# Down projections with the residual added in halves, an earlier bias table, and the last K and Q parts kept in pages

## The chip, the cores and the metric

The kernel runs on one core of one Trainium2 chip. The metric is the device time of one execution in microseconds (us). TensorE does the matrix products and is called PE in the profile, VectorE is DVE, ScalarE is ACT, GpSimd is POOL, and SyncE, which here only issues DMAs, is SP. A DMA issued from POOL goes through a queue of its own; on the way it can add what it reads to what already stands at the destination, which this kernel uses for the residual.

## The reference

A trunk of two layers over a residual stream `x` of 1024 positions by 1024 channels, all in float32:

```python
for i in range(2):
    h = rms_norm(x, mix_norm[i])
    x = x + (short_conv_mixer(h, ...) if i == 0 else dilated_attention_mixer(h, ..., rel_bias))
    x = x + swiglu(rms_norm(x, ffn_norm[i]), w_gate[i], w_up[i], w_down[i])   # 2816 hidden channels
return rms_norm(x, final_norm)

def swiglu(h, w_gate, w_up, w_down):
    return (jax.nn.silu(h @ w_gate) * (h @ w_up)) @ w_down
```

The attention has 16 heads of 64 and three dilated windows whose outputs are mixed by their log-denominators; each score gets a bias, looked up in the 32x16 table `rel_bias` by distance. FFN0 below is the feed-forward part of layer 0, FFN1 that of layer 1.

## The kernel before

**Numbers as pairs.** Every float32 operand is split in a rounded part `hi` and a rest `lo`, and each product is three matmuls: hi·hi, hi·lo, lo·hi (L612, L613, L614 in `mm`). ACT writes hi (L157 for weights, L604 for activations), DVE then subtracts to get lo (L158, L605). L225 on DVE forms the sums of weight blocks that the scheme below needs.

**Seven products.** The large projections use a seven-product scheme (class `Strassen`). PE does one product after another into one of eight banks; the order of all instructions is written by hand (the program is scheduled by the order of its code), so every engine works its own list in that order and waits by semaphores.

**The down projection.** `down(c, feed)` does chunk `c` of the hidden channels; both feed-forward parts have three chunks here (some tiles are done apart). Chunk by chunk it goes through the products m = 1, 2, 6, 7, 4, 5, 3, and within each through k = 0, 2, 4, 6. Each (m, k) is 9 or 12 matmuls of 128x512 (three for each tile of the chunk: three tiles or four), and its bank is added to one half of one tile of the result, `X[n]` (128x1024, half 0 or 1). m = 1 and 2 go to half 0 of X0, X2, X4, X6; m = 6 and 3 to half 1 of these; m = 4 to half 0 of X1, X3, X5, X7; m = 7 and 5 to half 1 of these. In chunk 0 the first bank for a half is copied by ACT (L836: m = 1, 6, 7, 4) and the second added by DVE (L839: m = 2, 5, 3); in the later chunks DVE adds all of them (L839). So in chunk 0 the half 0 of X0, X2, X4, X6 is complete after m = 2, half 0 of X1, X3, X5, X7 after m = 4, and the other halves after m = 5 and m = 3.

**The residual.** The x of before the feed-forward part lies in DRAM (`source`, called `spill` in the trace). In chunk 0, POOL adds it to a finished X tile by an accumulating DMA (L854). `feed` loads the hidden activations (`hin`, L813 on SP) and splits them for the products to come; `take` does the same for the weights (`raw`, L188 on SP), four products ahead.

**The bias tables.** `bias_tables` is a generator in three steps: (1) DVE fills `rel`, POOL clears and loads five small tiles (`oh` and `rel`, L541 to L549); (2) ACT and DVE split `rel`; (3) PE multiplies them into four banks (L560), ACT and DVE add the two halves of each bank (L561, L562), and the result goes to DRAM (`tables`). `after(m, k)` calls one step at each of three places in the last chunk of FFN0. In the same places `ready_half` squares and splits finished halves of X for the next phase (L1182, L923, L924).

**The Q/K phase.** After FFN0 the Q and K projections run pair by pair (8 pairs). `emit` scales a finished 128x512 part on DVE (L1197, L1199), splits it (ACT L1202, DVE L1205) and stores both pieces to DRAM through POOL (`kq`, L1203 and L1206). While the last of these are stored, PE does the first value tiles of the attention (L1578 to L1580).

**Memory.** Tiles of 128x1024 come from a ring of 41 `page`s that lives all through the kernel. Tiles of 128x512 (`half_page`) come from a pool that is opened anew for each of three stages: the pool of the first stage is closed after the Q/K phase, and the second pool takes its memory. What is loaded into tiles of the second pool (the `bias` tiles of L1529, and behind them on SP's list `ka`, `qa`, `ql`, L1606 to L1612) therefore waits for whoever still uses a half page of the first. PE's first scores (L1634, L1635) read `kca` (made by ACT from `ka`, L1618), `qa` and `ql`.

Of the kernel before, what the change touches and what calls it, by code (L numbers as in the profile page):

```python
# [11 lines left out]
F32R = mybir.dt.float32r  # L12
AF = mybir.ActivationFunctionType
ALU = mybir.AluOpType
# [9 lines left out]
HALF = 512  # L24
# [30 lines left out]
QK_PAIRS = 8  # L55
# [58 lines left out]
def trunk(ctx: ExitStack, tc: tile.TileContext, x, gains_in, cwi, ck, cwo, wqkv, wo, relb,  # L114
          wg, wu, wd, oneh, ident, out):
    nc = tc.nc
# [6 lines left out]
    def page(name, dt=F32):  # L123
        return pages.tile([128, 1024], dt, name=name, tag="page", bufs=PAGES)
# [3 lines left out]
    def half_page(name, dt=F32):  # L128
        return scope["pool"].tile([128, 512], dt, name=name, tag="half", bufs=scope["halves"])

    def bank():
        return psum.tile([128, 512], F32, name="bank", tag="bank")

    def half(h):
        return slice(h * HALF, (h + 1) * HALF)
# [302 lines left out]
    X = [None] * KT  # L438
# [140 lines left out]
    class Strassen:  # L579
# [248 lines left out]
        def down(self, c, feed):  # L828

            p, r, done = {}, {}, set()  # L830

            def add(n, h, b):
                if c == 0 and (n, h) not in done:
                    if X[n] is None:
                        X[n] = page("x")
                    nc.scalar.activation(X[n][:, half(h)], b, AF.Copy)  # L836
                    done.add((n, h))
                else:
                    nc.vector.tensor_tensor(out=X[n][:, half(h)], in0=X[n][:, half(h)], in1=b, op=ALU.add)  # L839

            for i, m in enumerate(DOWN):
                d = c + (i + 2) // len(DOWN)
                steps = range(len(self.chunks[d])) if d < len(self.chunks) else (0, 2)
                for k in range(0, KT, 2):
                    if m == 1:
                        p[k] = bank()
                    if m == 5:
                        r[k] = bank()
                    b = bank() if m == 2 else r[k] if m in (3, 5) else p[k]
                    self.mm((c, k), m, b, m in (1, 2, 5), 4)  # L850
                    n, h = k + (m in (5, 7, 4)), int(m in (6, 5, 7, 3))
                    add(n, h, b)
                    if c == 0 and m in (5, 3):
                        nc.gpsimd.dma_start(out=X[n], in_=self.source[n], accum_op=ALU.add)  # L854
                    if m == 4:
                        del p[k]
                    if k // 2 in steps:
                        next(feed, None)
                    self.downed(c, m, k)

        def downed(self, c, m, k):
            pass
# [301 lines left out]
    class QueryKey(Conv):  # L1164
# [28 lines left out]
        def emit(self, p, part, h, v):  # L1193

            t, rstd = half_page("kq"), self.norm.rstd[:, half(h)]
            if part == 1:
                nc.vector.tensor_tensor(out=by_time(t), in0=by_residue(v), in1=by_residue(rstd), op=ALU.mult)  # L1197
            else:
                nc.vector.scalar_tensor_tensor(t, v, 0.125, rstd, op0=ALU.mult, op1=ALU.mult)  # L1199
            yield  # L1200
            hi, lo, to = half_page("kq_hi", F32R), half_page("kq_lo", F32R), self.kq[p, part]
            nc.scalar.activation(hi, t, AF.Copy)  # L1202
            nc.gpsimd.dma_start(to[:128, half(h)], hi.bitcast(F32))  # L1203
            yield
            nc.vector.tensor_tensor(out=lo, in0=t, in1=hi, op=ALU.subtract)  # L1205
            nc.gpsimd.dma_start(to[128:, half(h)], lo.bitcast(F32))  # L1206
# [89 lines left out]
    class Swiglu(Strassen):  # L1296
# [111 lines left out]
                    self.storing.pop(0)  # L1408

        def downed(self, c, m, k):  # L1410
            if self.after and c + 1 == len(self.chunks):
                self.after(m, k)

        def feed_forward(self, stats, last_step, after, final=None):
            prep, self.after = [], after

# [554 lines left out]
    with tc.tile_pool(name="first", bufs=1) as scope["pool"]:  # L1971
        scope["halves"] = 20
        conv = Conv(Norm(0))
        sw, group1, *rest = into_ffn(0, Norm(2))
        conv.mix(group1)
        norm = Norm(1)
        qk = QueryKey(norm)
        tab = bias_tables()

        def after(m, k):  # L1980
            if (m, k) in ((1, 0), (1, 4), (2, 2)):
                next(tab, None)
            if m in (2, 4, 5, 3):
                qk.ready_half(k + (m in (4, 5)), int(m in (5, 3)), (m, k) in ((2, 0), (5, 0)))
            if m == 3:
                combos[QK, k // 4]((6, 7)[k // 2 % 2])

        sw.feed_forward(*rest, after)
        qk.mix()
# [123 lines left out]
```

## Time and profile before

| | |
|---|---|
| time, median of 3 runs | 2102.26 us (2100.35 to 2102.6) |
| the profiled execution: its time / its span | 2099.16 us / 2097.4 us |
| mean granted PE clock | 0.998 |
| PE busy | 2074.3 us, 99% |
| DVE busy | 1759.1 us, 84% |
| ACT busy | 1027.7 us, 49% |
| POOL busy | 256.0 us, 12% |
| DMA queues: SP's / POOL's share of 16 engines' span | 32.3% / 13.2% |
| FFN0 chunk 0 to 1 / FFN1 chunk 0 to 1 | around 801 / around 1924 us |
| bias tables on PE / first scores of the attention | 893 to 898 / 1136 to 1142 us |

Times in the rows are microseconds from the start of the span. Matmuls are pipelined: the profile gives each 128x512 matmul 0.39 us, but when nothing holds PE they start 0.227 us apart (the stretch from 1893 to 1925 has 143 of them), so lost time on PE is read from how many matmuls a stretch holds, and not from the busy share alone. In a row of the timeline the number in brackets is how long the engine stood idle before it, and what ended that.

### The profile page before, as it was taken

Reading aid. Unit: us, or ns where it says so; the run is one execution under the profiler, and the core shown is the slowest. Engines: PE = TensorE matmul, PEld = TensorE weight load, DVE = VectorE, ACT = ScalarE, POOL = GpSimd, SP = SyncE. Lnnn points to the kernel's source line nnn. Section 1 sums busy time; section 2 is a strip of 40 time slices with the busy share of each in tenths; the row PEclk is TensorE's granted clock in tenths of the full one; section 3 lists DMA queues with packets and bytes.
Section 4 is the critical chain, followed back from the end, with each engine's and each line's share of the span. In section 5 each row is a group of like instructions: output and inputs, shape, how many; then the busy total and the mean of one; then the engine's idle time right before and its main releaser. Section 6 shows DMA issues by size and latency. Waiting matters only on the chain.

```text
span 2097.4 us, 30780 instructions
## 1 busy us (share of the span) xinstructions
PE 2074.3 (99%) x10954; PEld 1785.2 (85%) x10954; DVE 1759.1 (84%) x3302; ACT 1027.7 (49%) x1902; POOL 256.0 (12%) x365
## 2 busy tenths in 40 slices
PE   9999999999999999999999999999999999999998
PEld 7888888888888888878889999998888888887787
DVE  8898769988888887888975888987998888896996
ACT  8433427443444563456543666655544444354443
POOL 1000000110101001010322333211001010001000
PEclk9999999999999999999999999999999999999999
DMA  7322643323323567552757867955223333368532
GB/s 221 96 96 71 236 133 74 106 101 111 109 99 109 174 221 198 174 143 106 241 179 211 195 175 216 244 182 139 81 86 109 100 109 103 114 216 211 162 101 81
DMA packets 131624, 305.69 MB, mean 146 GB/s; under 512 B 15324, under 2 KB 46126, under 8 KB 131472
## 3 DMA queue, kind: packets, MB, share of 16 engines
q1 hardware_dynamic: 96128, 203.51, 32.3%
q0 software_dynamic: 27712, 85.52, 13.2%
q10 hardware_dynamic: 7632, 14.70, 1.9%
q8 instruction: 87, 1.43, 0.3%
q14 instruction: 65, 0.53, 0.1%
HBM read 209.99 MB, written 84.50 MB: 140 GB/s over the span
## 4 chain that ended last, share of the span: by engine, by line
PE 84%; DVE 6%; issue 4%; DMA 2%; POOL 1%; ACT 1%; SPq 0%; POOLq 0%; DVEq 0%; ACTq 0%
PE bank L612 18%; PE bank L614 18%; PE bank L613 18%; PE bank L1709 5%; PE bank L415 3%; PE bank L417 3%; PE bank L416 3%; PE bank L704 3%; PE bank L707 3%; PE bank L706 3%; DMA x<-spill 2%; PE bank L1635 1%; PE bank L1634 1%; PE bank L1578 1%; PE bank L1580 1%
## 5 line engine op out<-in xcount | busy, mean ns | idle before, releaser
L614 PE MATMUL bank<-b,w 128*128 128x512 f32 x2064 | 805.0, 390 | 5.1 <-DVE w L158 4.7
L612 PE MATMUL bank<-b,w 128*128 128x512 f32 x2064 | 804.5, 390 | 3.4 <-ACT w L157 1.7
L613 PE MATMUL bank<-b,w 128*128 128x512 f32 x2064 | 804.0, 390 | 0.4 <-DVE b L924 0.3
L614 PEld LDWEIGHTS bank<-b,w 128*128 128x128 f32 x2064 | 387.4, 188 | 92.7 <-DVE w L158 11.8
L612 PEld LDWEIGHTS bank<-b,w 128*128 128x128 f32 x2064 | 387.6, 188 | 83.6 <-ACT w L157 2.4
L613 PEld LDWEIGHTS bank<-b,w 128*128 128x128 f32 x2064 | 387.6, 188 | 79.9 <-DVE b L924 1.3
L157 ACT ACTIVATE w<-combo 128x512 fp32r<-128x512 f32 (+2 forms) x496 | 258.9, 549 | 267.7 <-DVE combo L225 250.8
L158 DVE TENSOR_TENSOR w<-combo,w 128x512 fp32r<-128x512 f32 (+2 forms) x496 | 286.4, 590 | 32.9 <-ACT w L157 32.6
L618 ACT ACTIVATE part<-bank 128x512 f32<-128x512 f32 x192 | 114.5, 596 | 393.6 <-PE bank L614 390.2
L158 DVE TENSOR_TENSOR w<-raw,w 128x512 fp32r<-128x512 f32 (+2 forms) x340 | 190.6, 582 | 36.8 <-ACT w L157 36.6
L622 DVE TENSOR_TENSOR part<-part,bank 128x256 f32<-128x256 f32 (+1 forms) x372 | 174.9, 499 | 34.7 <-PE bank L614 18.6
L157 ACT ACTIVATE w<-raw 128x512 fp32r<-128x512 f32 (+2 forms) x340 | 171.2, 536 | 26.9 <-PE bank L707 10.5
L415 PE MATMUL bank<-w_hi,w 128*128 128x512 f32 (+1 forms) x336 | 126.2, 376 | 0.0
L839 DVE TENSOR_TENSOR x<-x,bank 128x512 f32<-128x512 f32 x136 | 92.8, 683 | 38.7 <-DMA x<-spill 19.2
L416 PE MATMUL bank<-w_lo,w 128*128 128x512 f32 (+1 forms) x336 | 124.2, 370 | 0.0
L417 PE MATMUL bank<-w_hi,w 128*128 128x512 f32 (+1 forms) x336 | 124.1, 369 | 0.0
L225 DVE TENSOR_TENSOR combo<-raw 128x512 f32<-128x512 f32 (+1 forms) x176 | 116.0, 660 | 0.0
L605 DVE TENSOR_TENSOR b<-hin,b 128x512 fp32r<-128x512 f32 x140 | 95.3, 685 | 15.5 <-ACT b L604 15.4
L534 DVE TENSOR_TENSOR x<-x,bank 128x512 f32<-128x512 f32 (+1 forms) x88 | 55.7, 635 | 41.4 <-PE bank L417 40.6
L604 ACT ACTIVATE b<-hin 128x512 fp32r<-128x512 f32 x140 | 86.0, 618 | 2.6 <-PE bank L614 1.4
L707 PE MATMUL bank<-b,w 128*128 128x256 f32 x288 | 81.5, 283 | 0.0
L706 PE MATMUL bank<-b,w 128*128 128x256 f32 x288 | 81.5, 283 | 0.0
(229 smaller groups left out, 3310.5 us busy)
## 6 DMA issues: line engine op xcount, KB each, us to landing
hin<-part SPq DMA_DIRECT2D x140, 256.0 KB, 3.8
raw<-in_ffn_w_gate SPq DMA_DIRECT2D x44, 512.0 KB, 3.7
raw<-in_ffn_w_up SPq DMA_DIRECT2D x44, 512.0 KB, 3.7
part<-sum POOLq DMA_DIRECT2D x80, 256.0 KB, 2.3
raw<-in_attn_w_qkv SPq DMA_DIRECT2D x27, 512.0 KB, 4.0
raw<-in_conv_w_in SPq DMA_DIRECT2D x24, 512.0 KB, 4.2
raw<-in_ffn_w_down SPq DMA_DIRECT2D x32, 384.0 KB, 5.0
part<-part POOLq DMA_DIRECT2D x40, 256.0 KB, 2.5
```

What stands on the lines that cost most here:

```text
L157: nc.scalar.activation(hi, src, AF.Copy)
L158: low = lambda: eng.tensor_tensor(out=lo, in0=src, in1=hi, op=ALU.subtract)
L225: eng.tensor_tensor(out=c, in0=a, in1=b, op=op)
L415: nc.tensor.matmul(b, whi[:, a], ahi[:, s], start=first, stop=False)
L416: nc.tensor.matmul(b, whi[:, a], alo[:, s], start=False, stop=False)
L417: nc.tensor.matmul(b, wlo[:, a], ahi[:, s], start=False, stop=last)
L612: nc.tensor.matmul(b, hi[:, a], bhi, start=start and k == 0, stop=False, skip_group_check=True)
L613: nc.tensor.matmul(b, hi[:, a], blo, start=False, stop=False, skip_group_check=True)
L614: nc.tensor.matmul(b, lo[:, a], bhi, start=False, stop=k == n - 1, skip_group_check=True)
L622: nc.vector.tensor_tensor(out=t, in0=t, in1=b, op=ALU.add)
L706: nc.tensor.matmul(b, hi[:, a], blo, start=False, stop=False, skip_group_check=True)
L707: nc.tensor.matmul(b, lo[:, a], bhi, start=False, stop=k == n - 1, skip_group_check=True)
```

## The change

Three edits; the arithmetic stays the same.

1. In chunk 0 of each down projection, the residual is added in halves of 128x512, each right after the product that completes the half, and no longer in tiles of 128x1024 after m = 5 and m = 3.
2. The first step of `bias_tables` moves from the last chunk's (1, 0) to (3, 2) of the chunk before, the second from (1, 4) to (1, 2), the third from (2, 2) to (2, 0). For this `after` now gets the chunk too, counted back from the last.
3. In `emit`, the hi and lo pieces of the last Q/K pair lie in the two halves of a page, and no longer in two half pages.

```diff
@@ down
-                    if c == 0 and m in (5, 3):
-                        nc.gpsimd.dma_start(out=X[n], in_=self.source[n], accum_op=ALU.add)
+                    if c == 0 and m in (2, 4, 5, 3):
+                        nc.gpsimd.dma_start(out=X[n][:, half(h)], in_=self.source[n][:, half(h)], accum_op=ALU.add)
@@ emit
-            hi, lo, to = half_page("kq_hi", F32R), half_page("kq_lo", F32R), self.kq[p, part]
+            to = self.kq[p, part]
+            if p == QK_PAIRS - 1:
+                w = page("kq_w", F32R)
+                hi, lo = w[:, :HALF], w[:, HALF:]
+            else:
+                hi, lo = half_page("kq_hi", F32R), half_page("kq_lo", F32R)
@@ downed
-            if self.after and c + 1 == len(self.chunks):
-                self.after(m, k)
+            if self.after:
+                self.after(c + 1 - len(self.chunks), m, k)
@@ the call in layer 0
-        def after(m, k):
-            if (m, k) in ((1, 0), (1, 4), (2, 2)):
+        def after(c, m, k):
+            if (c, m, k) in ((-1, 3, 2), (0, 1, 2), (0, 2, 0)):
                 next(tab, None)
+            if c < 0:
+                return
```

What this does to the order of instructions, at three places. First POOL's list at chunk 0 of FFN0, before (`spill_77` to `spill_84` are the residuals of X0 to X7, `part` a store of the stage before):

```order
L784 DMA part_10_4_240<-sum 128x512
L854 DMA x<-spill_78 128x1024
L854 DMA x<-spill_80 128x1024
L854 DMA x<-spill_82 128x1024
L854 DMA x<-spill_84 128x1024
L854 DMA x<-spill_77 128x1024
L854 DMA x<-spill_79 128x1024
```

And now (first the halves after m = 2, then those after m = 4, then the first of those after m = 5; the others of m = 5 and the four of m = 3 follow):

```order
L784 DMA part_10_4_240<-sum 128x512
L854 DMA x<-spill_77 128x512
L854 DMA x<-spill_79 128x512
L854 DMA x<-spill_81 128x512
L854 DMA x<-spill_83 128x512
L854 DMA x<-spill_78 128x512
L854 DMA x<-spill_80 128x512
L854 DMA x<-spill_82 128x512
L854 DMA x<-spill_84 128x512
L854 DMA x<-spill_78 128x512
```

Eight DMAs became sixteen of half the size, and X0's, which stood fifth, now begins the list. FFN1 reads the same.

Second, DVE's list where the bias tables are made, before:

```order
L158 TENSOR_TENSOR w<-combo,w 128x512
L839 TENSOR_TENSOR x<-x,bank 128x512
L605 TENSOR_TENSOR b<-hin,b 128x512
L924 SCALAR_TENSOR_TENSOR b<-x,gains,b 128x512
L225 TENSOR_TENSOR combo<-raw 128x512
L225 TENSOR_TENSOR combo<-combo,raw 128x512
L158 TENSOR_TENSOR w<-combo,w 128x512
L839 TENSOR_TENSOR x<-x,bank 128x512
L605 TENSOR_TENSOR b<-hin,b 128x512
L562 TENSOR_TENSOR t_8374<-bank,low 16x512
L562 TENSOR_TENSOR t_8374<-bank,low 16x201
```

And now:

```order
L158 TENSOR_TENSOR w<-combo,w 128x512
L839 TENSOR_TENSOR x<-x,bank 128x512
L605 TENSOR_TENSOR b<-hin,b 128x512
L562 TENSOR_TENSOR t_8350<-bank,low 16x512
L562 TENSOR_TENSOR t_8350<-bank,low 16x201
```

One product's share of DVE's work (L924 to L605) has moved from ahead of L562 to behind it; on PE the four L560 stand 12 matmuls sooner.

Third, POOL's list at the end of the Q/K phase, before (`kq_0_2937` and `kq_1_2938` are Q and K of the last pair):

```order
L1203 DMA kq_1_2936<-kq_hi 128x512
L1206 DMA kq_1_2936<-kq_lo 128x512
L1203 DMA kq_0_2937<-kq_hi 128x512
L1206 DMA kq_0_2937<-kq_lo 128x512
L1203 DMA kq_1_2938<-kq_hi 128x512
L1206 DMA kq_1_2938<-kq_lo 128x512
L1546 MEMSET ql_10357 64x1024
```

And now:

```order
L1208 DMA kq_1_2936<-kq_hi 128x512
L1211 DMA kq_1_2936<-kq_lo 128x512
L1208 DMA kq_0_2937<-kq_w 128x512
L1211 DMA kq_0_2937<-kq_w 128x512
L1208 DMA kq_1_2938<-kq_w 128x512
L1211 DMA kq_1_2938<-kq_w 128x512
L1551 MEMSET ql_10361 64x1024
```

The order is the same; the last four transfers now read from pages, so the last one that reads a half page is the `kq_lo` of the pair before.

## The prediction

> **What bounds the kernel now.** PE is busy for 99% of the span, so only the places where PE waits can give time back. I read the list of waits first, for whom PE waited (us in total, times, longest), then the table by stretches, for how many matmuls the suspected ones hold, and then the timeline at each place.
>
> ```profile
> PE bank L614 <- DVE w L158: 4.7, 8, 1.3
> PE bank L560 <- issue: 2.5, 1, 2.5
> PE bank L1635 <- DMA raw<-in_attn_w_qkv: 1.7, 1, 1.7
> PE bank L612 <- DVE t L562: 0.8, 1, 0.8
> PE bank L1634 <- ACT kca L1618: 0.5, 1, 0.5
> ...
> 1925.00:1957.00 32.00, 29.27 (x121) 21.55 (x120) 23.35 (x43) 8.70 (x18) 0.00 (x0) 1.00 0.64 148
> 1957.00:1989.00 32.00, 32.00 (x143) 26.48 (x142) 29.51 (x54) 15.17 (x32) 0.00 (x0) 1.00 0.63 205
> 803.00:835.00 32.00, 31.61 (x137) 25.04 (x136) 23.37 (x38) 7.26 (x13) 0.00 (x0) 1.00 0.65 162
> 893.00:906.00 13.00, 9.71 (x43) 7.70 (x42) 11.37 (x23) 9.23 (x19) 2.14 (x4) 1.00 0.38 93
> ```
>
> In the lower rows the stretch comes first, then its length, then busy time (and instructions) of PE, PEld, DVE, ACT, POOL, then the granted clock. An undisturbed 32 us holds 143 matmuls, 0.227 us apart. The start of FFN1's second chunk (1925 on) holds 22 fewer, 5.0 us; that of FFN0 (803 on) 6 fewer, 1.4 us. The bias tables' 13 us hold 39 large matmuls and four L560 where 58 belong: 19 × 0.227 = 4.3, less some 0.6 of L560's own work, 3.7 us. The attention's start loses 3.9 us (below). Together 14.0 us, the most that this change can touch.
>
> **Residual in halves.** DVE is what PE waits for at the chunk crossings, and DVE itself waits for the residual's DMAs. Its waits from 780 to 830 and from 1924 to 1960, its timeline there, and the longest PE wait behind it:
>
> ```profile
> DVE x L839 <- DMA x<-spill: 9.8, 3, 7.1
> ...
> DVE x L839 <- DMA x<-spill: 9.4, 4, 7.6
> ...
> 808.80 0.69 DVE L839 TENSOR_TENSOR x<-x,bank 128x512 f32<-128x512 f32 x1 [7.11 <-DMA x<-spill]
> ...
> 1931.72 0.69 DVE L839 TENSOR_TENSOR x<-x,bank 128x512 f32<-128x512 f32 x1 [7.65 <-DMA x<-spill]
> ...
> 1934.26 0.69 DVE L839 TENSOR_TENSOR x<-x,bank 128x512 f32<-128x512 f32 x1 [0.78 <-DMA x<-spill]
> ...
> 1936.72 0.69 DVE L839 TENSOR_TENSOR x<-x,bank 128x512 f32<-128x512 f32 x1 [0.71 <-DMA x<-spill]
> ...
> 1939.60 0.50 PE L614 MATMUL bank<-b,w 128*128 128x512 f32 x1 [1.20 <-DVE w L158]
> ```
>
> Chunk 1's first add was due at 808.80 − 7.11 = 801.7 in FFN0 and 1931.72 − 7.65 = 1924.1 in FFN1. DVE works in order: behind the add stand L605 and L158, and these make PE late. The add touches half 0 of X0 alone, whose residual now leaves some 40 us sooner. Half 1 is first wanted at m = 6, eight products later: 801.7 + 8 × 2.72 = 823.5 (12 matmuls each) and 1924.1 + 8 × 2.04 = 1940.4 (9 matmuls). Are the halves there by then?
>
> ```profile
> x<-spill POOLq DMA_DIRECT2D x16, 512.0 KB, 13.5
> acc<-sq POOLq DMA_DIRECT2D x15, 256.0 KB, 3.8
> acc<-sq POOLq DMA_DIRECT2D x6, 512.0 KB, 5.1
> ...
> DMA to landing us min/median/max: 3.3/4.1/6.6
> ...
> 786.75 0.90 POOL L854 DMA_DIRECT2D x<-spill  x1 [38.19 <-DMA raw<-in_ffn_w_down]
> ...
> L836 ACT ACTIVATE x<-bank x7: 598/598/600, 771.2 to 783.5; 128x512 f32<-128x512 f32 x7
> L836 ACT ACTIVATE x<-bank x6: 598/598/598, 1896.4 to 1906.6; 128x512 f32<-128x512 f32 x6
> ```
>
> The first three rows are DMA issues (KB each, median us to landing), the fourth all landings of the 256 KB accumulating DMAs of L1187. Queued 512 KB residuals land about 2.5 us apart (the DVE rows 1931.72, 1934.26, 1936.72). The halves are half the bytes; between the two sizes of `acc<-sq` lie 5.1 − 3.8 = 1.3 us. So I take 1.3 to 1.6 us for a queued half, 3.3 to 6.6 us for one alone. The last m = 4 copies start at 783.5 and 1906.6, so these four leave from about 777 and 1900; 12 halves in line from there take 12 × 1.6 = 19 us and are through by 796 and 1919, or, since the last of them leave only as chunk 1 begins (801 and 1924), some 4 us after that; due are 823 and 1940. POOL pays eight more issues of 0.90 us in each FFN, where it stood idle for 38 us. What follows once this wait is gone: chunk 1's DVE work on its own. The crossing to chunk 2 has the same adds and splits and no residual, and its row (1957 on) has the full 143. So the gain is 5.0 + 1.4 = 6.4 us; bounds 0 (DVE turns out too slow anyway) and 6.4.
>
> **Bias tables.** PE's and DVE's timelines, and ACT's:
>
> ```profile
> 893.46 0.74 PE L560 MATMUL bank<-oh,rel 128*128 128x512 f32 x3
> 896.70 0.35 PE L560 MATMUL bank<-oh,rel 128*128 128x256 f32 x1 [2.50 <-issue]
> 897.85 0.50 PE L612 MATMUL bank<-b,w 128*128 128x512 f32 x1 [0.79 <-DVE t L562]
> ...
> 891.85 0.68 DVE L839 TENSOR_TENSOR x<-x,bank 128x512 f32<-128x512 f32 x1
> ...
> 895.92 0.68 DVE L839 TENSOR_TENSOR x<-x,bank 128x512 f32<-128x512 f32 x1
> ...
> 897.12 1.83 DVE L562 TENSOR_TENSOR t<-bank,low 16x512 f32<-16x512 f32 x4
> ...
> 892.56 0.72 ACT L923 ACTIVATE b<-x,gains 128x512 fp32r<-128x512 f32 x1 [3.11 <-DVE x L839]
> ```
>
> Three of the four find a free bank. The fourth needs the one that DVE's L839 empties (895.92 + 0.68 = 896.60), and the next product needs one that L562 empties. So the loss follows DVE's distance from PE: the add starts 895.92 − 893.46 = 2.46 us after the first L560. One product sooner, the L560s start at 893.46 − 2.72 = 890.74, and the add ahead of them on DVE is the one at 891.85: 1.11 us. L562 stands as far behind its add as before (after L605), and ACT, idle for 3.11 us there, has L561 done in time. Gain 2.46 − 1.11 = 1.35 us. The first step, moved by three products, only fills tiles sooner on POOL and DVE; PE did not wait for these. The five half pages that it takes are held longer, so SP's `hin` loads use others; the waits above show none for `hin`. Bounds: 0 (DVE falls behind by as much) and 3.7 (all). I take 1.35, since both times are rows.
>
> **Last Q/K parts in pages.** SP, POOL, the chain, PE, DVE, and the chain's pace at 1139 and 1143:
>
> ```profile
> 1125.58 0.75 SPq L1529 DMA_DIRECT2D bias<-tables  x1
> ...
> 1115.26 0.54 POOL L1206 DMA_DIRECT2D kq<-kq_lo  x1 [1.25 <-DVE kq_lo L1205]
> ...
> 1120.80 4.47 DMA kq<-kq_lo
> ...
> 1136.33 0.36 PE L1634 MATMUL bank<-qa,kca 128*128 128x256 f32 x1 [0.52 <-ACT kca L1618]
> 1138.37 0.55 PE L1635 MATMUL bank<-ql,kca 128*128 128x256 f32 x1 [1.68 <-DMA raw<-in_attn_w_qkv]
> ...
> 1118.55 0.69 DVE L1205 TENSOR_TENSOR kq_lo<-kq,kq_hi 128x512 fp32r<-128x512 f32 x1 [0.24 <-ACT kq_hi L1202]
> ...
> 1138.92 0.21 PE bank L1634
> 1142.75 0.12 PE bank L1634
> ...
> 1120.00:1126.00 6.00, 6.00 (x52) 6.00 (x52) 0.00 (x0) 0.95 (x2) 1.71 (x4) 1.00 0.37 134
> 1136.00:1140.00 4.00, 1.99 (x9) 1.85 (x9) 0.61 (x2) 0.70 (x2) 2.15 (x4) 0.78 1.04 262
> ```
>
> SP's first load into the second pool left at 1125.58, when the last `kq_lo` (issued 1120.80) had landed. The ones behind it end in `ql`, which PE's L1635 wanted (the trace names the weight load issued right behind it). After that wait PE's steps are 0.21 us and not 0.12 for 3.2 us, and the granted clock is 0.78 in the stretch. Loss: 0.52 + 1.68 + 0.43 for the slow first matmul + 3.0 × (1 − 0.12/0.21) = 1.3, so 3.9 us. Now the load waits for the `kq_lo` issued at 1115.26 and for DVE's last reading of a half page, 1118.55 + 0.69 = 1119.24: some 6 us sooner. `ql` would be there at 1132.4 and not 1138.4, and PE asks at 1136.33 − 0.52 = 1135.8. What may eat the 3.4 us between: the loads now run beside the stores of the last pair, which fill 0.37 of the DMA engines from 1120 to 1126, 2.2 us of their time. That leaves 1.2 us. Gain 3.9; bounds 0 and 3.9. The Trainium skill, "TensorE: Matmul & The Clock Gate", section "Why this matters for your kernels", wants idle gaps above some 3 us before the clock halves; here 0.52 and 1.68 us were enough, while the 2.50 at 896.70 were followed by full clock, so the measurement decides. By the page the slow steps would stay, and the sum be lower by 1.3 (2092.3 for 2091.0).
>
> **Sum.** 6.4 + 1.35 + 3.9 = 11.6 us. The profiled execution, 2099.16, would become 2087.5. It lies below all three timed runs; against their median it is 2102.26 − 11.6 = 2090.7, and I say 2091.0.
>
> **Rivals.**
> 1. *DVE or the loads take the place of a wait.* DVE needs a wider lead than chunk 1 gives, or `ql` still comes late, or DVE's distance at the bias tables stays 2.46 us. For it: DVE is busy 29.51 of 32 us at the second crossing, and `ql` has 1.2 us to spare. Against: 143 matmuls there. With half of the halves' gain and the tables' lost: 2102.3 − 3.2 − 3.9 = 2095.
> 2. *It does not do what it says.* The residuals are late because the queue is full of weights, whatever their size, and the second pool waits for something else. Only the tables' 1.35 is left: 2101. Against: POOL stood idle for 38 us before the first.
> 3. *Slower: small accumulating DMAs are not quicker in line.* If queued halves land p us apart, the 12 from 777 and 1900 last until 777 + 12p and 1900 + 12p, while the last ones wanted at m = 6 are due at 823.5 + 3 × 2.72 = 831.7 and 1946.5. PE then loses 24p − 101 in both. It ends slower by 0.2% once this passes 6.4 + 1.35 + 3.9 + 4.2 = 15.9, so from p = 4.9; with p = 6.6, the longest one alone, 2102 − 11.6 + 57 = 2148; I put it at 2108. Against: 512 KB already land 2.5 apart. The Trainium skill, "DMA: Bandwidth & Descriptors", section "Anatomy of one DMA — SWDGE (gpsimd) path", has 2.0 us fixed for each and bytes/436e3 on top, an estimate of 2.6 us for 256 KB one by one; no run here shows that for halves, and it too stays under 4.9.
>
> **Chances.** The sum (gain 9.3 to 13.8): 0.60. Rival 1 (4.8 to 9.3): 0.25. Rival 2 (within 4.2, which is 0.2%, about what a measurement of this kernel can tell): 0.11. Rival 3: 0.04. Range 2088.0 (nearly all 14.0) to 2097.5 (4.8), with 0.85 inside; faster 0.85, same 0.11, slower 0.04.
>
> **What would show it.** After: no L839 waiting for `x<-spill` around 801 and 1924, and about 143 matmuls in the 32 us from there; the fourth L560 within 1.9 us of the first and L612 about 3 after it; the first L1529 around 1119 on the old clock, no wait at L1635, granted clock 1.00 in those four microseconds. Wrong if the matmul counts there stay low with the waits gone from DVE, if `ql` is still waited for, or if PE waits for weights (`raw`) or `hin` in places where it did not.

## The result, and the profile after

The changed kernel takes 2087.52 us (median of 6 runs, 2087.18 to 2089.48) where the kernel before, timed beside it, takes 2101.37 (6 runs, 2100.23 to 2102.6). The ratio is 0.9935, 95% interval 0.9923 to 0.9948: 13.9 us faster, by the interval 10.9 to 16.2. The prediction was 2091.0, and its range ended at 2088.0, 0.5 us above the median, which lies outside it: the direction and the places were right, the amount was too small.

The profiled execution of the changed kernel takes 2087.8 us, its span is 2086.0. Against the profiled execution of before, 2099.16, that is 11.4 us, close to the predicted sum (11.6). So the two traces differ by about what was forecast, and the timed runs by 2.5 us more. Where those come from is the main question below.

The first five rows of the changed kernel's list of PE's waits (us in total, times, longest); the two waits at the first scores are gone from the list, and L614's wait for w is 3.0 us and not 4.7 (2.5 of the 3.0 lie in the first 100 us):

```profile
PE bank L614 <- DVE w L158: 3.0, 3, 1.9
PE bank L612 <- ACT w L157: 1.6, 1, 1.6
PE bank L560 <- issue: 1.1, 1, 1.1
PE bank L1973 <- DVE ones L1967: 1.0, 1, 1.0
PE bank L612 <- DVE t L562: 0.8, 1, 0.8
```

Its table by stretches, for FFN0's crossing, FFN1's, the bias tables and the first scores, and the first load into the second pool on SP:

```profile
801.00:833.00 32.00, 32.00 (x143) 26.50 (x142) 29.18 (x48) 11.21 (x20) 0.86 (x1) 1.00 0.61 174
1919.00:1951.00 32.00, 32.00 (x143) 26.51 (x142) 30.62 (x56) 13.78 (x28) 0.00 (x0) 1.00 0.63 190
888.00:901.00 13.00, 11.14 (x50) 8.87 (x49) 11.55 (x24) 7.89 (x16) 1.00 (x2) 1.00 0.25 70
1136.00:1140.00 4.00, 4.00 (x36) 4.00 (x35) 3.55 (x8) 0.00 (x0) 0.79 (x2) 1.00 1.05 188
...
1117.26 0.75 SPq L1534 DMA_DIRECT2D bias<-tables  x1
```

Both crossings hold the full 143 matmuls (137 in FFN0 and 121 in FFN1 before); the tables' 13 us hold 46 large ones where 39 were; the 4 us at the first scores hold 36 matmuls at full clock, where 9 stood at 0.78. The first load leaves at 1117.26 and not at 1125.58.

DVE's waits at the two crossings (780 to 830 and 1915 to 1955) name the residual no more, only ACT and PE:

```profile
DVE b L605 <- ACT b L604: 3.3, 3, 1.5
DVE x L839 <- PE bank L614: 2.8, 4, 0.8
...
DVE x L839 <- PE bank L614: 3.4, 8, 0.9
```

And PE at the tables, the predicted picture to the tenth (fourth L560 1.81 us after the first, L612 2.95 after it):

```profile
890.17 0.74 PE L560 MATMUL bank<-oh,rel 128*128 128x512 f32 x3
891.98 0.35 PE L560 MATMUL bank<-oh,rel 128*128 128x256 f32 x1 [1.07 <-issue]
893.12 0.50 PE L612 MATMUL bank<-b,w 128*128 128x512 f32 x1 [0.79 <-DVE t L562]
```

### The profile page after: what moved, and what is told of

The parts are those of the page before. It is cut to its first block, busy times and chain, and to the rows that moved or that the text cites. A ratio compares the mean times of both kernels' runs of the same rounds, so it can differ in the third digit from the quotient of the medians.

```text
span 2086.0 us, 30813 instructions
## 1 busy us (share of the span) xinstructions
PE 2069.0 (99%) x10954; PEld 1784.5 (86%) x10954; DVE 1760.0 (84%) x3302; ACT 1027.9 (49%) x1902; POOL 269.8 (13%) x381
## 4 chain that ended last, share of the span: by engine, by line
PE 94%; DVE 3%; ACT 1%; issue 0%; DMA 0%; DVEq 0%; ACTq 0%
PE bank L612 21%; PE bank L614 21%; PE bank L613 21%; PE bank L1714 5%; PE bank L415 3%; PE bank L416 3%; PE bank L417 3%; PE bank L707 3%; PE bank L704 3%; PE bank L706 3%; PE bank L1583 2%; PE bank L1585 1%; PE bank L1584 1%; PE bank L1640 1%; PE bank L1639 1%; DVE b L605 0%
## 5 line engine op out<-in xcount | busy, mean ns | idle before, releaser
L612 PE MATMUL bank<-b,w 128*128 128x512 f32 x2064 | 804.4, 390 | 3.0 <-ACT w L157 1.6
L614 PE MATMUL bank<-b,w 128*128 128x512 f32 x2064 | 804.0, 390 | 3.1 <-DVE w L158 3.0
L614 PEld LDWEIGHTS bank<-b,w 128*128 128x128 f32 x2064 | 387.5, 188 | 86.9 <-DVE w L158 6.1
L612 PEld LDWEIGHTS bank<-b,w 128*128 128x128 f32 x2064 | 387.7, 188 | 83.1 <-ACT w L157 2.0
L605 DVE TENSOR_TENSOR b<-hin,b 128x512 fp32r<-128x512 f32 x140 | 95.2, 685 | 15.6 <-ACT b L604 15.5
```

Source lines behind the costliest of these rows:

```text
L612: nc.tensor.matmul(b, hi[:, a], bhi, start=start and k == 0, stop=False, skip_group_check=True)
L614: nc.tensor.matmul(b, lo[:, a], bhi, start=False, stop=k == n - 1, skip_group_check=True)
```

## The experiments

For every trace, PE's loss at a place is worked out in the same way: the distance from each matmul's start to the next one's, less the distance that its form has undisturbed (0.227 us for 128x512, 0.120 for 128x256, 0.112 for 128x128), added up over the place. In us:

| kernel (its span) | crossing FFN0 | bias tables | attention's start | crossing FFN1 |
|---|---|---|---|---|
| before (2097.4) | 1.3 | 3.7 | 3.9 | 4.9 |
| before, second trace (2099.0) | 1.4 | 5.3 | 4.0 | 4.5 |
| tables alone (2098.4) | 1.8 | 3.9 | 4.5 | 4.1 |
| pages alone (2096.6) | 2.1 | 6.4 | -0.2 | 4.3 |
| halves alone (2089.4) | -0.1 | 6.3 | -0.2 | -0.1 |
| without the pages (2085.3) | -0.1 | 2.3 | -0.2 | -0.1 |
| without the tables' move (2088.9) | -0.1 | 6.3 | -0.2 | -0.1 |
| without the halves (2092.5) | 1.6 | 2.3 | -0.2 | 4.8 |
| halves, late (2092.0) | 0.3 | 5.3 | -0.2 | 2.4 |
| POOL memsets (2094.8) | 1.3 | 5.3 | 0.8 | 5.1 |
| changed (2086.0) | -0.1 | 2.3 | -0.2 | -0.1 |
| changed, second trace (2087.1) | -0.1 | 3.9 | -0.2 | -0.1 |
| tables one by one (2084.5) | -0.1 | 0.2 | -0.2 | -0.1 |
| tables one by one, second trace (2083.2) | -0.1 | 0.2 | -0.3 | -0.1 |

Elsewhere only the first 100 us move from trace to trace, between 8.1 and 9.8, whatever the kernel.

### Each part alone, and before once more

The edits are the three parts of the diff, each put alone into the kernel before.

*Halves alone.*

> Only the residual in halves (both feed-forward parts). The traces of before and after differ by 11.4 us, the timed medians by 13.9; 2.4 us are unexplained. Theory 1 (the excess is made at the attention's start, whose loss differs from execution to execution): this kernel is 6.4 us faster than before, as the matmul counts say, so about 2095.0. Theory 2 (the excess is made at the two chunk crossings, where the landings differ): 8.8 us faster, about 2092.6. Theory 3 (the profiled execution of before was simply a quick one, and the excess lies at no place of the change): 6.4. In its trace, whatever the theory: no DVE wait for the residual, 143 matmuls in the 32 us after both crossings, and the losses at the bias tables (3.7) and at the attention's start (3.9 by the first trace; more than that by theory 1).

Measured: 2091.08 us (5 runs, 2090.01 to 2091.4), before 2101.27 (27 runs); ratio 0.9948, interval 0.9936 to 0.9960, 10.2 us. None of the three theories gave so much. The crossings give their 6 us, and the attention's start loses nothing either, though this kernel keeps the half pages. The tables' loss is 6.3 us and not 3.7.

*Tables alone.*

> Only the bias tables' steps moved. All theories: 1.4 us faster than before, about 2100.0. In its trace the crossings and the attention's start are as before; by theory 1 the loss at the attention's start is not always 3.9 us but in most executions 5 to 7, by theory 2 the crossings lose more than 6.4 in all.

Measured: 2099.12 us (11 runs, 2097.14 to 2102.09), ratio 0.9989 (0.9980 to 0.9998), 2.2 us; the interval, 0.4 to 4.2 us, holds the forecast 1.4 too. In its trace the clock fell behind the shorter gap as well, and the tables lose 3.9 us.

*Pages alone.*

> Only the last Q/K pair's pieces in pages. Theory 1: 6.3 us faster than before, about 2095. Theory 2 and 3: 3.9 us faster, about 2097.5. In its trace no wait at the first scores and full clock there; the crossings lose 6.4 (theory 2: more).

Measured: 2098.04 us (11 runs, 2095.11 to 2101.27), ratio 0.9981 (0.9972 to 0.9990), 3.2 us. The attention's start loses nothing, as predicted; the tables lose 6.4 us in its trace.

*Before once more.*

> The kernel before, unchanged: no difference in time, and a second trace of it. Theory 1: its loss at the attention's start is not the 3.9 us of the first trace but 5 to 7. Theory 2: the crossings lose more than 6.4. Theory 3: the losses at the places of the change are within 0.5 us of those of the first trace, and a longer span has its excess elsewhere.

Measured: 2101.32 us (11 runs), ratio 1.0001. Its losses at the crossings and the attention's start are those of the first trace within half a microsecond; at the tables it loses 1.6 us more. All three theories looked at the wrong place. What differs is the granted clock behind L560. The stretches of before (first trace), then of before's second trace, then of the pages alone:

```profile
892.00:896.00 4.00, 2.20 (x11) 1.57 (x9) 3.77 (x7) 3.41 (x7) 0.00 (x0) 1.00 0.01 4
896.00:900.00 4.00, 2.51 (x10) 1.99 (x11) 3.52 (x10) 2.05 (x4) 0.50 (x1) 1.00 0.31 84
900.00:904.00 4.00, 4.00 (x19) 3.31 (x18) 3.27 (x6) 2.43 (x5) 1.41 (x2) 1.00 0.73 179
...
896.00:900.00 4.00, 2.15 (x7) 1.61 (x8) 3.87 (x10) 2.15 (x4) 0.50 (x1) 0.86 0.29 80
900.00:904.00 4.00, 4.00 (x14) 3.21 (x13) 2.92 (x6) 2.68 (x6) 1.42 (x2) 0.72 0.64 168
...
896.00:900.00 4.00, 1.34 (x3) 0.98 (x4) 4.00 (x8) 2.94 (x6) 0.39 (x1) 0.76 0.14 13
900.00:904.00 4.00, 4.00 (x11) 3.03 (x11) 2.79 (x8) 2.77 (x7) 1.53 (x3) 0.50 0.66 207
```

PE's gaps are the same in all three (2.5 us, then 0.7 to 0.8), and the third column from the end, the clock, stays at 1.00 in the first only. In the last, 900 to 904 has 11 matmuls where 19 belong. The first trace was the exception: of seven traces with the tables' steps in their old place, six lose 5.3 to 6.4 us there and one 3.7.

The changes of the clock recorded in the traces show why. Within each trace they lie whole multiples of 3.413 us apart, and each stretch at half clock, the one at the kernel's end left aside, is 3.41 or 6.83 us long: the clock is set window by window. Here are the same three traces, cut at the borders of these windows (PE's busy time stands right behind the length):

```profile
892.48:895.90 3.42, 1.72 (x9) 1.16 (x7) 3.19 (x6) 3.31 (x7) 0.00 (x0) 1.00 0.02 5
895.90:899.31 3.41, 1.82 (x7) 1.42 (x8) 3.32 (x9) 1.89 (x3) 0.50 (x1) 1.00 0.21 73
899.31:902.72 3.41, 3.41 (x16) 2.81 (x15) 2.28 (x6) 2.69 (x6) 1.41 (x2) 1.00 0.68 172
...
895.44:898.85 3.41, 1.00 (x4) 0.75 (x5) 3.41 (x7) 2.46 (x5) 0.14 (x1) 1.00 0.07 23
898.85:902.26 3.41, 3.41 (x10) 2.64 (x9) 2.23 (x8) 2.40 (x7) 1.07 (x3) 0.50 0.62 158
...
894.68:898.09 3.41, 0.91 (x5) 0.54 (x4) 3.38 (x6) 2.72 (x6) 0.00 (x0) 1.00 0.01 5
898.09:901.50 3.41, 2.71 (x7) 1.94 (x8) 2.68 (x8) 2.12 (x5) 0.50 (x1) 0.50 0.48 114
901.50:904.91 3.41, 3.41 (x10) 2.64 (x9) 2.92 (x6) 2.19 (x5) 1.41 (x2) 0.50 0.63 175
```

Counted over the 14 traces of the table, 14 windows at full clock hold at most 1.67 us of busy PE, and every one is followed by a window at half clock; the other 8483 hold 1.70 us or more, and none is. The windows lie differently against the program in each execution: in the first trace a border (895.90) happens to fall into the gap of 2.5 us, so that neither of its two windows is idle enough, and in the other six one window takes most of the idle time. Where the second gap falls into the halved window, that one is not busy enough either (2.62 to 2.75 us, three traces), and the next is halved too. So the price comes in steps: 1.6 us for one halved window, 2.6 to 2.7 for two.

### The changed kernel less one part

Each run puts one part of the diff back to what the kernel before has: `emit` (without the pages), `downed` and `after` (without the tables' move) or the accumulating DMA (without the halves).

*Without the pages.*

> The changed kernel with the last Q/K pieces in half pages again. The trace of the halves alone shows no loss at the attention's start: there POOL's third-last store of a Q/K piece begins 1.1 us sooner after its releaser (2.29 and not 3.42 us of idle time before it). Theory P (POOL pauses some 1.5 us at fixed places of its own program; eight more instructions move the pause away from that store, and this alone lets the first loads come in time): as fast as the changed kernel, 2087.5, and no wait at the first scores. Theory Q (the pages are what removes the loss there): 4 us slower than the changed kernel, about 2091.5.

Measured: 2087.65 us (5 runs, 2087.01 to 2089.74), ratio 0.9936, as fast as the changed kernel. So beside the halves the pages are worth nothing that shows. The reason is in POOL's list. The last three stores of Q/K pieces and what waits for them, before and without the pages:

```profile
1119.73 0.54 POOL L1206 DMA_DIRECT2D kq<-kq_lo  x1 [3.40 <-DVE kq_lo L1205]
1120.26 0.54 POOL L1203 DMA_DIRECT2D kq<-kq_hi  x1
1120.80 0.54 POOL L1206 DMA_DIRECT2D kq<-kq_lo  x1
1125.63 1.95 POOL L1546 MEMSET ql<- 64x1024 f32 x2 [4.29 <-DMA kq<-kq_lo]
...
1115.93 0.54 POOL L1206 DMA_DIRECT2D kq<-kq_lo  x1 [2.29 <-DVE kq_lo L1205]
1116.47 0.54 POOL L1203 DMA_DIRECT2D kq<-kq_hi  x1
1117.00 0.54 POOL L1206 DMA_DIRECT2D kq<-kq_lo  x1
1120.16 1.95 POOL L1546 MEMSET ql<- 64x1024 f32 x2 [2.62 <-DMA kq<-kq_lo]
```

The wait before the first of the three is 1.1 us shorter, and the wait for the last one to land is 4.29 before and 2.62 now. Together 2.8 us, more than PE's waits there were (0.52 and 1.68), and the halved clock behind them goes with them.

*Without the tables' move.*

> The changed kernel with the bias tables' steps where they were. The tables' loss was 3.7 us in the first trace of before, but 5.3, 6.4 and 6.3 in three later ones, where the granted clock went to 0.5 behind L560; with the steps moved it was 2.3 (clock 1.00) and 3.9 (clock down to 0.64). Theory K (the old gap nearly always halves the clock for a while, the shorter one seldom): 3.2 to 4.0 us slower than the changed kernel, about 2091, and a loss of 5 to 6.5 us there in its trace. Rival (the predicted 1.4 us): 2088.9.

Measured: 2090.65 us (5 runs, 2088.28 to 2092.14), 3.1 us slower than the changed kernel was; the tables lose 6.3 us in its trace, with the clock at 0.50 from 896 to 900. That is what theory K forecast. The medians alone do not exclude the predicted 1.4 (the ratio, 0.9936 to 0.9961, overlaps the changed kernel's); the loss in the trace, with two halved windows, speaks against it.

*Without the halves.*

> The changed kernel with the residual in whole tiles after m = 5 and m = 3 again. POOL's program up to the last Q/K stores is then that of before, its pause falls on the third-last store as there, and the pages take that store off the path: crossings lose 6 us as before, tables 2.3 to 3.9, attention's start nothing. 6.2 us slower than the changed kernel, about 2093.9. If the pages did nothing even with the pause in place: 2098.

Measured: 2094.81 us (6 runs, 2094.28 to 2095.33), ratio 0.9966 (0.9954 to 0.9978), 7.3 us slower than the changed kernel's first runs and 6.1 slower than its five runs timed beside this one (2088.71); 6.2 were forecast. POOL's wait before the third-last store is 3.40 us again, as before, and the pages keep it from costing anything.

### Halves without being sooner

```diff
                     if c == 0 and m in (5, 3):
-                        nc.gpsimd.dma_start(out=X[n], in_=self.source[n], accum_op=ALU.add)
+                        for g in range(2):
+                            nc.gpsimd.dma_start(out=X[n][:, half(g)], in_=self.source[n][:, half(g)], accum_op=ALU.add)
```

> The kernel before, with each residual tile added by two half DMAs, both issued where the whole one was (after m = 5 and m = 3). Theory P: eight more instructions on POOL are enough to move its pause, so the attention's start loses nothing (no wait at the first scores), 4 us faster than before, less whatever 16 DMAs land later than 8: the crossings lose 6 to 9 us, the time is 2097 to 2100. Theory Q: no gain at the attention's start; 2101 or more. If being sooner were not what helps at the crossings but being small, the crossings would lose nothing: 2091 to 2095.

Measured: 2094.33 us (5 runs, 2093.63 to 2095.44), ratio 0.9968 (0.9955 to 0.9980), 6.5 us faster. The attention's start loses nothing, as theory P said, and the crossings lose 2.7 us, less than expected; the time lies below theory P's range and in that of halves that help by being small. DVE still waits for the residual at both crossings (8.9 us in FFN0, 7.0 in FFN1; 9.8 and 9.4 before):

```profile
DVE x L839 <- DMA x<-spill: 8.9, 3, 6.1
...
DVE x L839 <- DMA x<-spill: 7.0, 4, 4.9
```

Half the bytes in the first waited-for transfer shorten the first wait by 1.0 us in FFN0 (7.1 to 6.1) and 2.7 in FFN1 (7.6 to 4.9), and PE's loss from 6.2 us to 2.7; sending them sooner takes away the rest.

### What moves POOL's pause

```diff
                     if c == 0 and m in (5, 3):
+                        nc.gpsimd.memset(spare, 0.0)
                         nc.gpsimd.dma_start(out=X[n], in_=self.source[n], accum_op=ALU.add)
```

> The kernel before with one small POOL memset of a tile of its own (128x1) ahead of each residual DMA: eight more POOL instructions in each feed-forward part, nothing else. Theory P (POOL's pause of 1.4 us sits at a place of its program, not at a time or at a kind of work): the pause no longer falls on the third-last Q/K store, its idle time before it is 2.3 us and not 3.4, the first loads leave 2 us or more sooner and PE does not wait at the first scores: 4 us faster, about 2097. Rival (the halves' smaller transfers or their earlier places in the queue are what moved it): no difference, 2101.

Measured: 2100.5 us (11 runs, 2096.59 to 2102.42), ratio 0.9994 (0.9985 to 1.0003): no difference, and the pause did not move. Here are its third-last store, its last, and the wait behind that:

```profile
1120.82 0.54 POOL L1208 DMA_DIRECT2D kq<-kq_lo  x1 [3.40 <-DVE kq_lo L1207]
...
1121.88 0.54 POOL L1208 DMA_DIRECT2D kq<-kq_lo  x1
1125.26 1.95 POOL L1548 MEMSET ql<- 64x1024 f32 x2 [2.84 <-DMA kq<-kq_lo]
```

So theory P is wrong in its cause: eight more instructions do nothing; eight more DMAs (halves alone, halves late, without the pages) do move it. The pause goes with POOL's DMAs; whether with their number or their size was not tried apart, and what exactly sets it stays open. In this one execution the last store landed quickly all the same and only 0.8 us were lost at the attention's start; this execution was the quickest of the 11, and their median shows nothing of it.

### The tables one by one

```diff
             nc.vector.tensor_tensor(out=t[g][:H, c0 - g * G0:c1 - g * G0], in0=b[:H, :w], in1=low[:H, :w], op=ALU.add)
+            if c1 < NG:
+                yield
...
-            if (c, m, k) in ((-1, 3, 2), (0, 1, 2), (0, 2, 0)):
+            if (c, m, k) in ((-1, 3, 2), (0, 1, 2), (0, 1, 4), (0, 1, 6), (0, 2, 0), (0, 2, 2)):
```

> The changed kernel with the tables' third step cut in four: one L560 with its L561 and L562 behind each of four successive products, from (1, 4) to (2, 2). If the loss of 2.3 us left there comes from four banks being wanted at once, each L560 now finds a bank free and costs only its own 0.1 to 0.23 us: 2.3 us faster than the changed kernel (2.6 with its rare clock drops), about 2085.0, and no halved clock there. If DVE's distance is what counts, PE waits for L562 at each of the four: no gain, or some tenths lost.

Measured: 2086.22 us (5 runs, 2085.77 to 2086.44), ratio to before 0.9928 (0.9915 to 0.9942). Once more, with the changed kernel beside it:

> The changed kernel with the third step of the tables cut in four, once more, beside the changed kernel on the same chip: by the first run 1.3 us faster in the median (the traces: 2.1 us less lost at the tables, 0.4 to 0.5 more in the first 100 us, which the edit does not touch). If the 0.4 is only scatter of the start, 2 us faster here.

> The changed kernel once more, beside the next one: 2087.5, tables' loss 2.3, or 3.9 where the clock drops.

Measured: 2085.2 us (5 runs, 2084.98 to 2088.44), ratio to before 0.9924 (0.9911 to 0.9936); the changed kernel on the same chip 2088.71 (5 runs, 2087.29 to 2089.33), ratio 0.9936 (0.9923 to 0.9948). The four matmuls now stand apart, without a gap before any, and the clock stays whole (second trace of this kernel):

```profile
888.00:892.00 4.00, 4.00 (x19) 3.30 (x18) 3.97 (x8) 1.24 (x3) 0.50 (x1) 1.00 0.08 16
892.00:896.00 4.00, 4.00 (x20) 3.31 (x19) 3.91 (x7) 3.65 (x6) 0.00 (x0) 1.00 0.28 70
```

The tables' loss, 2.3 or 3.9 us, falls to 0.2 in both traces, which is 2.1 or 3.7 us less. In the medians it is 1.3 us the first time (against the changed kernel's first runs) and 3.5 the second (against those beside it); this version is the fastest here.

## Why the prediction was right and wrong

**Residual in halves, 6.4 us: right.** The losses at the crossings are 5.9 to 6.4 us in the traces of kernels with whole residuals (6.2 in the first), and -0.1 at each of the two crossings with the halves sent sooner: 6.1 to 6.6 us. No add waits for `x<-spill`, POOL's eight more issues cost nothing, and no wait for `raw` or `hin` has come up.

**Bias tables, 1.35 us: too small, and this is the step that failed.** Its geometry was right (2.46 us to 1.11; the traces that keep full clock go from 3.7 to 2.3). The term put the clock behind the gap at nothing, and the only ground for that stands in a sentence on another place: that the 2.50 us at 896.70 "were followed by full clock, so the measurement decides". That was one execution, in which a border of the clock's windows happened to split the gap. In six of seven traces with the old placing the clock fell, with 1.6 to 2.7 us more lost: 5.5 us in the mean of the seven, (3.7 + 5.3 + 5.3 + 5.3 + 6.3 + 6.3 + 6.4)/7. With the new placing five traces lose 2.3, 2.3, 2.3, 3.9 and 3.9, 2.9 in the mean. So the move is worth 2.6 us in the mean of these traces, and 3.1 by the medians where only it is taken back. Rival 1 looked for a loss in DVE's distance from PE; that distance came out as costed, and it was the clock behind the gap that made the place dearer.

**The base of the sum.** The profiled execution of before, 2099.16, lay under all the timed runs. I noted that and did not ask why. It lay there since its clock held at the tables, so it lacked the very loss that the change shortens. The range's low end, 2088.0, came from the 14.0 us of that execution; with the 5.5 us of the mean at the tables it would have been about 2086, and the median inside. Of the 3.5 us between 2091.0 and the median, 0.9 is that before took 2101.37 beside the change and not 2102.26, 0.3 is rounding, and 2.3 are gain beyond the 11.6, 1.3 to 1.8 of them at the tables; the rest lies within the interval. That the two traces differ by nearly the sum is in part luck: both were spared the halved clock at the tables, and the changed kernel's lost some 0.8 us more in the first 100 us, which no part of the change touches.

**Pages, 3.9 us: right alone, nothing beside the halves.** Alone they take the whole loss away (-0.2 is left of 3.9 to 4.5 in three traces with half pages). In the changed kernel the first load left 8.3 us sooner. All work stood 2.0 us sooner there (the last store that reads a half page began at 1113.27 and not at 1115.26), so 6.3 are its own where some 6 were forecast. What no rival had: the halves take the same loss away, through POOL's list. So the sum's parts overlap: by the medians they give alone 10.2 + 2.2 + 3.2 = 15.6 us, together 13.9. By places it adds up without overlap: crossings 6.4, tables 2.6, attention's start 4.1, 13.1 us, inside the interval of 10.9 to 16.2.

**Rival 3** did not come: no add waits for the halves, and the sixteen of FFN0 land 3.8 to 9.4 us after issue. Where halves do queue, in the trace of the late ones, they land mostly 1.2 to 2.1 us apart; 1.3 to 1.6 were taken, and the rival needed 4.9.

**The clock.** In these traces short gaps are enough to halve it: 0.5 to 1.1 and then 1.5 to 1.7 us at the attention's start in each of three traces, 2.50 and 0.79 at the tables in six of seven, and the shorter 1.07 and 0.79 in two of five. The Trainium skill, "TensorE: Matmul & The Clock Gate", section "Why this matters for your kernels", asks only that no idle gap pass some 3 us; the traces differ. Section "What's actually happening" of that page of the Trainium skill says that the gate looks at activity in windows that run on freely. The traces agree: their windows of 3.413 us lie differently in each execution, and the same gaps cost the clock in one and not in the next.

## What to carry to other kernels

A gap that costs the clock or not by where it falls against the clock's windows makes one trace a poor price list: when the profiled execution lies outside the timed runs, look for what it was spared before subtracting from it, and take two or three traces of the kernel before. Where an addend arrives by DMA, send each piece when its destination is complete, not when the whole tile is. And when one edit changes the number or the size of the DMAs on a queue, a stall somewhere later on that queue can move: take parts back one at a time before crediting them.

## What the hardware showed that was not expected

- The granted clock is set in windows of 3.413 us. In 14 traces a full-clock window with at most 1.67 us of busy PE was always followed by half clock (14 windows), one with 1.70 us or more never (8483); a halved window with 2.62 to 2.75 us was followed by another halved one (3), one with 3.05 us or more by full clock (14).
- So PE idle for 2.5 and then 0.8 us, with some 0.35 us of work between, let the granted clock fall in six of seven traces, in three of them for two windows; idle of 1.07 and 0.79 us did so in two of five.
- POOL's engine begins some of its DMAs 1.4 to 1.6 us after everything they wait for has ended, where others begin after some 0.3. DVE's subtraction for the third-last store of before ended at 1118.31 and POOL began it at 1119.73. It is the same store in every trace that has POOL's DMAs as before, with or without memsets between, and not that store where the residual is sent in halves. The distance between such pauses, counted in POOL's DMAs, is not even (101, 113, 193, 218 and 292 DMAs into the program of before), so what they count stays open.
- With that pause POOL waited 4.3 to 4.5 us for the last store to land in three traces and 2.8 in one; with the pause elsewhere 2.6 to 2.7 in three. Why it lands sooner then was not tried apart.
